# The expert stage in a hand-written instruction order, in a transformer block on one Trainium2 core

## The chip, the core and the metric

The kernel runs as one launch on one core of a Trainium2 chip. The metric is the device time of the launch in microseconds (us). Before the change three runs took 2419.74, 2420.95 and 2422.48 us; the median is 2420.95 us. Engines are named as in the profile: PE is the matrix engine (PEld its weight loads), DVE the vector engine, ACT the scalar engine, POOL the general-purpose engine, SP the engine that issues most DMAs.

## What is computed

The reference is one encoder layer on 1024 tokens of width 1024. The first part (three kinds of attention or recurrence, a merge and an output projection) isn't touched. The second part is a mixture of 16 experts, in which each expert chooses 128 tokens:

```python
def expert_choice_ffn(h, w_router, w_gate, w_up, w_down):
    affinity = jax.nn.softmax((h @ w_router).astype(jnp.float32), axis=-1)
    top_val, top_idx = lax.top_k(affinity.transpose(0, 2, 1), cap)          # cap = 128
    xe = jax.vmap(lambda hb, ib: hb[ib])(h, top_idx)
    act = jax.nn.silu(einsum(xe, w_gate)) * einsum(xe, w_up)                # 1024 -> 2048
    ye = einsum(act, w_down) * top_val[..., None]                           # 2048 -> 1024
    # scatter-add of ye to the rows top_idx; then x + that sum, and a final rms_norm
```

All tensors are float32. The three weight matrices of one expert hold 8 MB each, so the 16 experts read 384 pieces of 1 MB.

## The kernel before

**Arithmetic.** A float32 product is made of three matmuls in the type fp32r. Each operand is split into a high part (`hi`, a rounded copy, made by ACT) and a low part (`lo = raw - hi`, made by DVE), and high·high, low·high and high·low are added up in one PSUM bank (`mm3`, L220 to L223).

**Pieces.** The weights of one expert come in 24 pieces of 128 x 2048 numbers (1 MB): for each of four quarters `f` of the hidden width two pieces of the gate matrix `wg`, two of the up matrix `wu` and two of the down matrix `wd`. A piece is fetched by SP into one of 14 raw buffers (`RAWB`, `fetch`, L1068), ACT makes its high part `ewh` (L1212), DVE its low part `ewl` (L1213); there are four buffers for each (`SPLB`). A raw buffer comes free when the low part is done; a high or low buffer comes free when PE has read it for the last time. Each piece feeds 12 matmuls of 512 columns.

**A quarter.** `gate_up` (L1267) runs 24 matmuls of the gate into bank `g`; ACT puts Silu of it into `sg` (L1303); 24 matmuls of the up matrix go into bank `u`, and DVE multiplies `sg` by it (L1309). `down` (L1273) belongs to the quarter before: PE turns `sg` round in four 128 x 128 transposes (L1277), the result is split into `ah` and `al` (L217, L218), and 24 matmuls (L1285 to L1287) add to the two banks `y`. At the end of an expert DVE scales both banks into `ye` (L1291), and POOL adds it to rows of `acc` in DRAM by an indirect DMA (L1292). `load_x` (L1252) gathers the 128 tokens of the next expert by an indirect DMA (L1254), transposes them in two groups of four (L1261) and splits them into `xh`, `xl` (L1263, L1264).

**What sets the order.** The expert stage isn't under `tc.manual_schedule()`: a planner orders the instructions of each engine from the program order, its own estimates and the free buffers. The engines then run in that fixed order and wait for each other by semaphores. The planner put some matmuls of the up matrix between the transposes and the down matmuls, and mixed the two streams. Within a piece the three kinds of matmul follow each other for each `k`, so that high and low part are both in use until the piece ends.

**The end.** After the last expert's scatter the 1024 rows of `acc` are loaded in eight tiles (L1329), normed (`final_norm`, L1318: a sum of squares on ACT, a power on POOL, a scaling on DVE) and stored; the 128 rows of the last expert are gathered, completed, normed and stored again by an indirect DMA (L1331 to L1337).

Of the kernel before, what the change touches and what calls it, by code (L numbers as in the profile page):

```python
# [25 lines left out]
F32 = mybir.dt.float32  # L26
F32R = mybir.dt.float32r
# [9 lines left out]
D = 1024  # L37
# [110 lines left out]
def block_kernel(ctx: ExitStack, tc: tile.TileContext, T, out, dbg=None, upto=99):  # L148
# [73 lines left out]
        PE.matmul(out_, ll, rh, start=False, stop=False)  # L222
        PE.matmul(out_, lh, rl, start=False, stop=(k_ == K - 1))  # L223

# [510 lines left out]
    rctx.close()  # L735
    rps_ctx.close()

# [1 line left out]
    pre_ctx.close()  # L739
    pctx.close()  # L740
    yctx = ExitStack()
# [269 lines left out]
            split_to(*(v[:, k:k + WBK] for v in w), raw[:, k:k + WBK])  # L1011
        return w

# [201 lines left out]

    early = {(n, 0, f, b): piece(n, 0, f, b, G) for n, f, b in order[:SPLB]}

    def weights(n, e, f, b, **kw):
        w = early.pop((n, e, f, b), None) or piece(n, e, f, b)
        return [v.rearrange("p (a c) -> p a c", **kw) for v in w]  # L1220

    work = [affT, affw]
    for r in range(CAP // 8):
        a, b = work[r % 2], work[(r + 1) % 2]
# [19 lines left out]
    V.tensor_copy(tvT, pi[:, 0:NE])  # L1244
    mctx.close()

    # experts
    with tc.tile_pool(name="eps", bufs=1, space=PSUM, reuse_waits="tile") as ps:
        def bank(tag, bufs):
            return ps.tile([128, 512], F32, name=tag, bufs=bufs)  # L1250

        def load_x(e):  # L1252
# [3 lines left out]
            xh = ep.tile([128, KD, 128], F32R, name="xh", bufs=2)  # L1256
            xl = ep.tile([128, KD, 128], F32R, name="xl", bufs=2)
            for b in range(2):
                p = bank("tr", 2)
                for k in range(4):  # L1260
                    PE.transpose(p[:, k * 128:(k + 1) * 128], xe[:, (4 * b + k) * 128:(4 * b + k + 1) * 128], ident)  # L1261
                p4 = p.rearrange("p (k t) -> p k t", k=4)
                A.activation(xh[:, 4 * b:4 * b + 4], p4, AF.Copy)  # L1263
                V.tensor_sub(xl[:, 4 * b:4 * b + 4], p4, xh[:, 4 * b:4 * b + 4].bitcast(F32))  # L1264
            return xh, xl

        def gate_up(e, f, nm, x, p):  # L1267
            for b in range(2):
                wh, wl = weights(nm, e, f, b, a=4)
                for k in range(4):  # L1270
                    mm3(p, 4 * b + k, KD, x[0][:, 4 * b + k], x[1][:, 4 * b + k], wh[:, k], wl[:, k])

        def down(e, f, sg, py):  # L1273
            ds = [weights("wd", e, f, b, a=2) for b in range(2)]
            pt = bank("tr", 2)
            for k in range(4):
                PE.transpose(pt[:, k * 128:(k + 1) * 128], sg[:, k * 128:(k + 1) * 128], ident)  # L1277
            ah = ep.tile([128, 4, 128], F32R, name="ah", bufs=1)
            al = ep.tile([128, 4, 128], F32R, name="al", bufs=1)
            split_to(ah, al, pt.rearrange("p (k t) -> p k t", k=4))  # L1280
            for k in range(4):
                for n in range(2):
                    o = py[n]
                    rh, rl = [d[:, k % 2, n * 512:(n + 1) * 512] for d in ds[k // 2]]
                    PE.matmul(o, ah[:, k], rh, start=(f == 0 and k == 0), stop=False)  # L1285
                    PE.matmul(o, al[:, k], rh, start=False, stop=False)  # L1286
                    PE.matmul(o, ah[:, k], rl, start=False, stop=(f == 3 and k == 3))  # L1287
            if f == 3 and e + 1 < NE:
                ye = lv.tile([128, D], F32, name="ye")
                for n in range(2):  # L1290
                    V.tensor_scalar(ye[:, n * 512:(n + 1) * 512], py[n], tvT[:, e:e + 1], None, op0=OP.mult)  # L1291
                G.indirect_dma_start(out=acc[:, :], out_offset=bass.IndirectOffsetOnAxis(ap=idx[:, e:e + 1], axis=0),  # L1292
                                     in_=ye, in_offset=None, compute_op=OP.add)

        xs = load_x(0)
        pend = py = None
        for e in range(NE):
            x = xs
            for f in range(4):
                pg, pu = bank("g", 2), bank("u", 2)  # L1300
                gate_up(e, f, "wg", x, pg)
                sg = ep.tile([128, 512], F32, name="sg", bufs=2)
                A.activation(sg, pg, AF.Silu)  # L1303
                if pend:
                    down(*pend)
                if f == 0:
                    py = [bank("y", 2) for _ in range(2)]
                gate_up(e, f, "wu", x, pu)
                V.tensor_mul(sg, sg, pu)  # L1309
                if f == 1 and e + 1 < NE:  # L1310
                    xs = load_x(e + 1)
                pend = (e, f, sg, py)
        down(*pend)

        grow = lv.tile([128, D], F32, name="xe")
        A.dma_start(grow, bass.AP(tensor=T["gfin"].tensor, offset=T["gfin"].offset, ap=[[0, 128], [1, D]]))

        def final_norm(t):  # L1318
            ss = ep.tile([128, 2], F32, name="ss", bufs=4)
            A.activation(t[:, D:], t[:, 0:D], AF.Square, accum_out=ss[:, 0:1])  # L1320
            rinv_of(ss[:, 0:1], ss[:, 1:2], 1, 1.0 / D, 1e-6)
            V.scalar_tensor_tensor(t[:, D:], t[:, 0:D], ss[:, 1:2], grow, op0=OP.mult, op1=OP.mult)
            return t[:, D:]

        last = idx[:, NE - 1:NE]
        ts = []
        for i in range(8):
            ts.append(rawt())
            SP.dma_start(ts[i][:, 0:D], acc[i * 128:(i + 1) * 128, :])  # L1329
        tl = rawt()  # L1330
        G.indirect_dma_start(out=tl[:, 0:D], out_offset=None, in_=acc[:, :],  # L1331
                             in_offset=bass.IndirectOffsetOnAxis(ap=last, axis=0))
        stores = [SP.dma_start(out[0, i * 128:(i + 1) * 128, :], final_norm(ts[i])) for i in range(8)]
        for n in range(2):
            hs = slice(n * 512, (n + 1) * 512)
            V.scalar_tensor_tensor(tl[:, hs], py[n], tvT[:, NE - 1:NE], tl[:, hs], op0=OP.mult, op1=OP.add)
# [30 lines left out]
```

## Time and profile before

| | |
|---|---|
| median of three runs | 2420.95 us |
| profiled execution, first to last instruction | 2419.1 us |
| mean granted clock of PE | 0.984 |
| first gate matmul of the expert stage | 1251.44 us |
| last up matmul of the expert stage | 2394.00 us |
| read from DRAM in the whole run | 517.56 MB |

The profiled execution's own time is its span of 2419.1 us; no other time of that execution is recorded. It lies 1.85 us below the median of the runs. Rows of a timeline give start and duration in us, then engine, line, operation, output and inputs, and in brackets the idle time before it with what ended it. Starts of matmuls follow each other more closely than their durations, because matmuls are pipelined: the spacing of starts is what a matmul costs in a stream. Rows of a window give the busy time of PE, PEld, DVE, ACT and POOL, then PE's granted clock, the busy share of the 16 DMA engines and GB/s.

### The profile page before, as it was taken

The page shows a single profiled execution, that of the slowest core. Times are in us where ns is not written, and L with a number is a line of the kernel's source. Part 1 is how long each engine was busy: PE and PEld are TensorE (multiplying, and loading weights), DVE is VectorE, ACT ScalarE, POOL GpSimd, SP SyncE. Part 2 cuts the span into 40 slices and gives each one's busy share as a digit, 9 for nine tenths or more (in the row PEclk, how much of TensorE's full clock was granted, in tenths as well). Part 3 has the DMA queues.
Part 4 walks back from the last instruction along what each step waited for, and adds up shares of the span by engine and source line. Part 5 has one row for each costly group of instructions (what it writes and reads, how often), then busy time and mean ns, then how long its engine had stood idle before and what let it go on. Part 6 is the DMA issues. An engine that isn't in the chain of part 4 may idle for free.

```text
span 2419.1 us, 34315 instructions
## 1 busy us (share of the span) xinstructions
PE 2279.5 (94%) x12931; PEld 1819.1 (75%) x12931; DVE 1725.5 (71%) x2155; ACT 1334.0 (55%) x1616; POOL 592.8 (25%) x1187
## 2 busy tenths in 40 slices
PE   7999999999999989999939999999999999999997
PEld 6677788877778767778727777777777777777775
DVE  6556556655665488762378888888888888888887
ACT  6554333333343378522236776776767667767675
POOL 1000666766666243340140000000011101011001
PEclk9999999999999999999969999999999999999998
DMA  6435443444343331363769999999999999999894
GB/s 233 151 137 209 129 122 98 117 126 125 98 119 96 122 111 64 116 191 121 250 267 372 357 367 364 355 360 375 362 370 362 361 359 374 365 375 367 295 413 173
DMA packets 193910, 588.55 MB, mean 243 GB/s; under 512 B 53072, under 2 KB 97360, under 8 KB 144592
## 3 DMA queue, kind: packets, MB, share of 16 engines
q1 hardware_dynamic: 187120, 562.88, 64.0%
q0 software_dynamic: 4752, 17.30, 2.8%
q10 hardware_dynamic: 1872, 6.17, 0.7%
q8 instruction: 102, 1.67, 0.3%
q14 instruction: 64, 0.52, 0.1%
HBM read 517.56 MB, written 68.73 MB: 242 GB/s over the span
## 4 chain that ended last, share of the span: by engine, by line
PE 64%; DVE 21%; issue 5%; ACT 4%; DMA 2%; POOL 2%; SPq 0%; POOLq 0%; DVEq 0%; ACTq 0%
PE acc L695 12%; DVE ewl L1213 8%; PE u L223 5%; PE y L1286 4%; PE y L1285 4%; PE y L1287 4%; PE u L221 3%; PE u L222 3%; PE acc L221 3%; PE acc L223 3%; PE acc L222 3%; PE g L221 3%; PE g L223 3%; PE g L222 3%; ACT ewh L1212 2%
## 5 line engine op out<-in xcount | busy, mean ns | idle before, releaser
L1213 DVE TENSOR_TENSOR ewl<-raw,ewh 128x2048 fp32r<-128x2048 f32 x380 | 861.7, 2289 | 162.0 <-ACT ewh L1212 161.8
L1212 ACT ACTIVATE ewh<-raw 128x2048 fp32r<-128x2048 f32 x384 | 732.2, 1917 | 289.0 <-PE y L1286 149.4
L223 PE MATMUL u<-ewl,xh 128*128 128x512 f32 x512 | 206.3, 403 | 23.8 <-DVE ewl L1213 22.0
L1292 POOL DMA_INDIRECT acc<-ye,idx x15 | 40.0, 2666 | 768.3 <-DVE ye L1291 768.3
L695 PE MATMUL acc<-hlo,wh 128*128 128x512 f32 x560 | 225.6, 403 | 0.0
L695 PE MATMUL acc<-hhi,wh 128*128 128x512 f32 x560 | 225.1, 402 | 0.0
L695 PE MATMUL acc<-hhi,wl 128*128 128x512 f32 x560 | 225.0, 402 | 0.0
L551 POOL TENSOR_TENSOR tmul<-tinv,blk 96x60 f32<-96x60 f32 (+24 forms) x496 | 172.1, 347 | 151.8 <-DMA blk<-ldr 114.3
L221 PE MATMUL u<-ewh,xh 128*128 128x512 f32 x512 | 205.5, 401 | 0.0
L1285 PE MATMUL y<-ewh,ah 128*128 128x512 f32 x512 | 194.7, 401 | 8.6 <-ACT ah L217 8.6
L221 PE MATMUL g<-ewh,xh 128*128 128x512 f32 x512 | 201.2, 393 | 0.0
L1286 PE MATMUL y<-ewh,al 128*128 128x512 f32 x512 | 200.4, 391 | 0.8 <-DVE al L218 0.8
L1287 PE MATMUL y<-ewl,ah 128*128 128x512 f32 x512 | 199.9, 390 | 0.0
L222 PE MATMUL u<-ewh,xl 128*128 128x512 f32 x512 | 199.9, 390 | 0.0
L223 PE MATMUL g<-ewl,xh 128*128 128x512 f32 x512 | 199.9, 390 | 0.0
L222 PE MATMUL g<-ewh,xl 128*128 128x512 f32 x512 | 199.5, 390 | 0.0
L553 POOL TENSOR_TENSOR tinv<-tinv,tmul 96x60 f32<-96x60 f32 (+24 forms) x496 | 176.2, 355 | 38.9
L223 PEld LDWEIGHTS u<-ewl,xh 128*128 128x128 f32 x512 | 96.0, 188 | 67.2 <-DVE ewl L1213 49.5
L1285 PEld LDWEIGHTS y<-ewh,ah 128*128 128x128 f32 x512 | 92.4, 189 | 42.3 <-ACT ah L217 23.7
L218 DVE TENSOR_TENSOR wl<-wraw,wh 128x1024 fp32r<-128x1024 f32 (+1 forms) x60 | 76.1, 1269 | 65.1 <-ACT wh L217 65.0
L695 PEld LDWEIGHTS acc<-hlo,wh 128*128 128x128 f32 x560 | 106.2, 190 | 20.6
L695 PEld LDWEIGHTS acc<-hhi,wl 128*128 128x128 f32 x560 | 105.9, 189 | 20.2
(309 smaller groups left out, 4409.4 us busy)
## 6 DMA issues: line engine op xcount, KB each, us to landing
raw<-in_wg_dram SPq DMA_DIRECT2D x128, 1024.0 KB
raw<-in_wu_dram SPq DMA_DIRECT2D x128, 1024.0 KB
raw<-in_wd_dram SPq DMA_DIRECT2D x128, 1024.0 KB
wraw<-in_wt_dram SPq DMA_DIRECT2D x46, 512.0 KB
pt<-pz SPq DMA_DIRECT2D x16, 768.0 KB
pgt<-po SPq DMA_DIRECT2D x48, 256.0 KB
gt<-pgt SPq DMA_DIRECT2D x16, 768.0 KB
blk<-ldr SPq DMA_DIRECT2D x64, 96.0 KB
```

Source lines behind the costliest of these rows:

```text
L218: V.tensor_sub(lo, src, hi.bitcast(F32))
L221: PE.matmul(out_, lh, rh, start=(k_ == 0), stop=False)
L222: PE.matmul(out_, ll, rh, start=False, stop=False)
L223: PE.matmul(out_, lh, rl, start=False, stop=(k_ == K - 1))
L551: G.tensor_tensor(tm[:, 0:m, 0:n], tt[:, 0:m, j:j + 1].to_broadcast([4 * NB, m, n]), lt[:, j, None, j + 1:32].to_broadcast([4 * NB, m, n]) ...
L553: G.tensor_tensor(tt[:, 0:m, j + 1:32], tt[:, 0:m, j + 1:32], tm[:, 0:m, 0:n], op=OP.add)
L695: PE.matmul(p, l[:, k], r[:, k, s0:s0 + 512], start=(k == 0 and i == 0), stop=(k == KD - 1 and i == 2))
L1212: A.activation(hi, raw, AF.Copy)
L1213: eng.tensor_tensor(lo, raw, hi.bitcast(F32), op=OP.subtract)
L1285: PE.matmul(o, ah[:, k], rh, start=(f == 0 and k == 0), stop=False)
L1286: PE.matmul(o, al[:, k], rh, start=False, stop=False)
L1287: PE.matmul(o, ah[:, k], rl, start=False, stop=(f == 3 and k == 3))
```

## The change

Only the expert stage changes. It is now written out under `tc.manual_schedule()`, so each engine runs the instructions in program order. A list `seq` fixes the order of the 384 pieces: for each step `s_` (a quarter of an expert) two gate pieces, the two down pieces of the step before, two up pieces.

- **Order on PE in a step:** first gate piece; the four transposes of the `sg` of the step before; second gate piece; both down pieces of the step before; first up piece; second up piece. In the third quarter of an expert the two groups of transposes of the next expert's tokens stand ahead of the first and of the second up piece; the gather is issued in the second quarter.
- **Order within a piece:** the eight matmuls that read the high part, then the four that read the low part.
- **Splits by hand:** after the piece with number n, ACT's high part of piece n+4 is issued (`hi_of`), DVE's low part of piece n+3 (`lo_of`), and with it SP's fetch of piece n+17 (`load`).
- **Scaling:** half of `ye` is scaled by ACT, the other half by DVE.
- **End:** the eight loads of `acc` follow the last fetches. One tile is normed in the last step but one, three in the last step, four after the transposes of the last `sg`. The row of gains is fetched in the last but two.

The numbers of matmuls, transposes, splits, bytes and buffers are the same. The diff, cut to its core:

```diff
-        def gate_up(e, f, nm, x, p):
-            for b in range(2):
-                wh, wl = weights(nm, e, f, b, a=4)
-                for k in range(4):
-                    mm3(p, 4 * b + k, KD, x[0][:, 4 * b + k], x[1][:, 4 * b + k], wh[:, k], wl[:, k])
+    with tc.tile_pool(name="eps", bufs=1, space=PSUM, reuse_waits="tile") as ps, tc.manual_schedule():
+        def hi_of(n):
+            if n < len(seq) and seq[n] not in his:
+                his[seq[n]] = hi = ep.tile([128, 2048], F32R, name="ewh", bufs=SPLB)
+                A.activation(hi, raws[seq[n]], AF.Copy)
+        def lo_of(n):
+            if n < len(seq) and seq[n] not in los:
+                los[seq[n]] = lo = ep.tile([128, 2048], F32R, name="ewl", bufs=SPLB)
+                V.tensor_sub(lo, raws.pop(seq[n]), his[seq[n]].bitcast(F32))
+            load(n + RAWB)
+        def gate_up(key, p):
...
+            for k in range(4):
+                PE.matmul(p, xh[:, 4 * b + k], wh[:, k], start=(b == 0 and k == 0), stop=False)
+                PE.matmul(p, xl[:, 4 * b + k], wh[:, k], start=False, stop=False)
+            for k in range(4):
+                PE.matmul(p, xh[:, 4 * b + k], wl[:, k], start=False, stop=(b == 1 and k == 3))
+        def down(key, a, py):
...
+            for i, (l, r) in enumerate(((ah, wh), (al, wh), (ah, wl))):
+                for k in range(2):
+                    for n in range(2):
+                        PE.matmul(py[n], l[:, 2 * b + k], r[:, k, n * 512:(n + 1) * 512], ...)
+        def scaled(e, py):
+            A.activation(ye[:, 0:512], py[0], AF.Copy, scale=tvT[:, e:e + 1])
+            V.tensor_scalar(ye[:, 512:D], py[1], tvT[:, e:e + 1], None, op0=OP.mult)
...
+        for s_ in range(steps + 1):
+            if s_ < steps:
+                gate_up(seq[at], pg)
+            if s_:
+                for k in range(4):
+                    PE.transpose(pt[:, k * 128:(k + 1) * 128], sg[:, k * 128:(k + 1) * 128], ident)
+                split_to(*a, pt.rearrange("p (k t) -> p k t", k=4))
+            if s_ == steps:
+                finish(8 - len(stores))
+            if s_ < steps:
+                hi_of(at - 1 + SPLB)
+                lo_of(at - 2 + SPLB)
+                gate_up(seq[at], pg)
+                A.activation(sg, pg, AF.Silu)
+                hi_of(at - 1 + SPLB)
+                lo_of(at - 2 + SPLB)
+            if f == 1 and e + 1 < NE:
+                gather(e + 1)
+            if s_:
+                for b in range(2):
+                    down(seq[at], a, py)
+                    hi_of(at - 1 + SPLB)
+                    lo_of(at - 2 + SPLB)
+                if pf == 3 and pe + 1 < NE:
+                    scaled(pe, py)
...
+            if f == 2 and e + 1 < NE:
+                x_half(e + 1, 0)
+            if s_ < steps:
+                gate_up(seq[at], pu)
+                hi_of(at - 1 + SPLB)
+                lo_of(at - 2 + SPLB)
+                if s_ == steps - 1:
+                    finish(1)
+                if f == 2 and e + 1 < NE:
+                    x_half(e + 1, 1)
+                gate_up(seq[at], pu)
+                V.tensor_mul(sg, sg, pu)
+                hi_of(at - 1 + SPLB)
+                lo_of(at - 2 + SPLB)
```

(`at` goes up by one after each piece.)

More of the change, by code (lines that the diff above doesn't have):

```diff
@@ L1245, in block_kernel, with load, gather @@
     mctx.close()
-    with tc.tile_pool(name="eps", bufs=1, space=PSUM, reuse_waits="tile") as ps:
+    steps = NE * 4
+    seq = []
+    for s_ in range(steps + 1):
+        if s_ < steps:
+            seq += [("wg", *divmod(s_, 4), b) for b in range(2)]
+        if s_:
+            seq += [("wd", *divmod(s_ - 1, 4), b) for b in range(2)]
+        if s_ < steps:
+            seq += [("wu", *divmod(s_, 4), b) for b in range(2)]
+    raws, his, los = {}, {}, {}
+    for k_ in seq[:RAWB]:
+        if k_ in first:
+            raws[k_] = first.pop(k_)
+    for k_, (hi, lo) in early.items():
+        his[k_], los[k_] = hi, lo
+    ts = []
+    with tc.tile_pool(name="eps", bufs=1, space=PSUM, reuse_waits="tile") as ps, tc.manual_schedule():
         def bank(tag, bufs):
             return ps.tile([128, 512], F32, name=tag, bufs=bufs)
-        def load_x(e):
+        def load(n):
+            if n < len(seq):
+                if seq[n] not in raws and seq[n] not in his:
+                    raws[seq[n]] = fetch(*seq[n])
+            elif n - len(seq) < 8:
+                i = n - len(seq)
+                ts.append(rawt())
+                SP.dma_start(ts[i][:, 0:D], acc[i * 128:(i + 1) * 128, :])
+        def hi_of(n):
[7 more added lines that the diff above has]
+            load(n + RAWB)
+        def gather(e):
             xe = lv.tile([128, D], F32, name="xe")
@@ L1295, in block_kernel @@
[L1295 to L1312, printed above, removed]
@@ new lines, in down @@
+        def down(key, a, py):
+            _, e, f, b = key
+            ah, al = a
+            wh, wl = (v.pop(key).rearrange("p (a c) -> p a c", a=2) for v in (his, los))
+            for i, (l, r) in enumerate(((ah, wh), (al, wh), (ah, wl))):
+                for k in range(2):
+                    for n in range(2):
+                        PE.matmul(py[n], l[:, 2 * b + k], r[:, k, n * 512:(n + 1) * 512],
+                                  start=(f == 0 and b == 0 and i == 0 and k == 0), stop=(f == 3 and b == 1 and i == 2 and k == 1))
@@ new lines, in scaled, with gain @@
+        def scaled(e, py):
+            ye = lv.tile([128, D], F32, name="ye")
+            A.activation(ye[:, 0:512], py[0], AF.Copy, scale=tvT[:, e:e + 1])
+            V.tensor_scalar(ye[:, 512:D], py[1], tvT[:, e:e + 1], None, op0=OP.mult)
+            G.indirect_dma_start(out=acc[:, :], out_offset=bass.IndirectOffsetOnAxis(ap=idx[:, e:e + 1], axis=0),
+                                 in_=ye, in_offset=None, compute_op=OP.add)
+        def gain():
+            t = lv.tile([128, D], F32, name="xe")
+            A.dma_start(t, bass.AP(tensor=T["gfin"].tensor, offset=T["gfin"].offset, ap=[[0, 128], [1, D]]))
+            return t
@@ L1323, in final_norm @@
             return t[:, D:]
-        last = idx[:, NE - 1:NE]
[L1326 to L1333, printed above, removed]
+        stores = []
@@ new lines, in finish @@
+        def finish(n):
+            for _ in range(n):
+                i = len(stores)
+                stores.append(SP.dma_start(out[0, i * 128:(i + 1) * 128, :], final_norm(ts[i])))
+        xin = {}
+        gather(0)
+        for n in range(SPLB + RAWB):
+            load(n)
+        for b in range(2):
+            x_half(0, b)
+        last = idx[:, NE - 1:NE]
+        at = 0
+        sg = py = None
+        for s_ in range(steps + 1):
+            e, f = divmod(s_, 4)
+            pe, pf = divmod(s_ - 1, 4)
+            if s_ < steps:
+                pg = bank("g", 2)
+                gate_up(seq[at], pg)
+                at += 1
+            if s_:
+                pt = bank("tr", 2)
+                for k in range(4):
+                    PE.transpose(pt[:, k * 128:(k + 1) * 128], sg[:, k * 128:(k + 1) * 128], ident)
+                a = [ep.tile([128, 4, 128], F32R, name=n, bufs=1) for n in ("ah", "al")]
+                split_to(*a, pt.rearrange("p (k t) -> p k t", k=4))
+            if s_ == steps:
+                finish(8 - len(stores))
+            if s_ < steps:
+                hi_of(at - 1 + SPLB)
+                lo_of(at - 2 + SPLB)
+                gate_up(seq[at], pg)
+                at += 1
+                sg = ep.tile([128, 512], F32, name="sg", bufs=2)
+                A.activation(sg, pg, AF.Silu)
[3 more added lines that the diff above has]
+                gather(e + 1)
+            if s_ == steps - 3:
+                grow = gain()
+            if s_:
+                if pf == 0:
+                    py = [bank("y", 2) for _ in range(2)]
+                for b in range(2):
+                    down(seq[at], a, py)
+                    at += 1
+                    hi_of(at - 1 + SPLB)
[3 more added lines that the diff above has]
+            if s_ == steps - 1:
+                tl = rawt()
+                G.indirect_dma_start(out=tl[:, 0:D], out_offset=None, in_=acc[:, :],
+                                     in_offset=bass.IndirectOffsetOnAxis(ap=last, axis=0))
+            if s_ >= steps - 2 and s_ < steps:
+                finish(s_ - steps + 3)
+            if f == 2 and e + 1 < NE:
+                x_half(e + 1, 0)
+            if s_ < steps:
+                pu = bank("u", 2)
+                gate_up(seq[at], pu)
+                at += 1
+                hi_of(at - 1 + SPLB)
+                lo_of(at - 2 + SPLB)
+                if s_ == steps - 1:
+                    finish(1)
+                if f == 2 and e + 1 < NE:
+                    x_half(e + 1, 1)
+                gate_up(seq[at], pu)
+                at += 1
+                V.tensor_mul(sg, sg, pu)
+                hi_of(at - 1 + SPLB)
+                lo_of(at - 2 + SPLB)
```

46 lines of the change are left out of this document (11 added, 35 removed).

## The prediction

> **What bounds the kernel now.** I read the engines' shares on the page first, then windows of one expert, then the waits, then the timelines of PE, DVE and ACT.
>
> ```profile
> PE 2279.5 (94%) x12931; PEld 1819.1 (75%) x12931; DVE 1725.5 (71%) x2155; ACT 1334.0 (55%) x1616; POOL 592.8 (25%) x1187
> ```
> ```profile
> 1766.00:1838.00 72.00, 70.52 (x315) 56.03 (x314) 61.61 (x37) 50.70 (x35) 6.46 (x2) 1.00 0.96 364
> ```
>
> In the window, one expert long, PE is busy for 70.5 of 72 us at a granted clock of 1.00, DVE for 61.6, ACT for 50.7; the DMA engines are 0.96 busy at 364 GB/s. PE looks full, but a matmul that is held up counts as busy. The expert's length comes from the scatters on POOL, its share of useful work from the spacing of matmul starts.
>
> ```profile
> 1766.27 3.38 POOL L1292 DMA_INDIRECT acc<-ye,idx  x1 [49.31 <-DVE ye L1291]
> ...
> 1981.33 3.38 POOL L1292 DMA_INDIRECT acc<-ye,idx  x1 [48.43 <-DVE ye L1291]
> ```
> ```profile
> 1857.32 0.60 PE L1261 MATMUL tr<-cst,xe 128*128 128x128 f32 x4
> 1857.68 0.48 PE L221 MATMUL g<-ewh,xh 128*128 128x512 f32 x1
> ...
> 1863.26 0.60 PE L1277 MATMUL tr<-cst,sg 128*128 128x128 f32 x4
> 1863.61 0.48 PE L221 MATMUL u<-ewh,xh 128*128 128x512 f32 x1
> 1863.93 0.39 PE L222 MATMUL u<-ewh,xl 128*128 128x512 f32 x1
> 1864.59 0.73 PE L1285 MATMUL y<-ewh,ah 128*128 128x512 f32 x2 [0.28 <-ACT ah L217]
> 1865.47 0.51 PE L223 MATMUL u<-ewl,xh 128*128 128x512 f32 x1
> ...
> 1866.28 0.39 PE L1286 MATMUL y<-ewh,al 128*128 128x512 f32 x1
> ...
> 1881.02 0.60 PE L1277 MATMUL tr<-cst,sg 128*128 128x128 f32 x4
> ```
>
> Three experts take 215.06 us, 71.69 each. A quarter, transposes to transposes, takes 1881.02 - 1863.26 = 17.76 us and has 72 matmuls. From 1866.28 on nothing is held up: 65 matmuls in 14.74 us, 0.2268 each. So 72 need 16.33, and 1.43 us are lost, all between 1863.26 and 1866.28: the transposes, then two up matmuls put in while ACT splits `ah`, a wait for `ah`, and an up matmul that waits for a low part. The waits of seven experts confirm the two releasers:
>
> ```profile
> ACT ewh L1212 <- PE y L1286: 81.0, 56, 2.2
> PEld u L223 <- DVE ewl L1213: 16.9, 28, 0.9
> PEld y L1285 <- ACT ah L217: 16.7, 28, 0.7
> ```
>
> Once in each of 28 quarters PE's weight load waits for each of them, 0.6 us a time. ACT itself waits for PE to give a high buffer back, not for a transfer: the stage is paced by PE and by the order of its stream.
>
> **The change: PE's stream.** Matmuls and transposes stay as many. The price of a group of four transposes is read where nobody waits: 0.36 us from 1857.32 to 1857.68, and the 24 gate matmuls behind it take 5.58 us (to 1863.26) instead of 24 x 0.2268 = 5.44; together 0.50. I take 0.50; the lower bound is 0.36, if the stream behind doesn't slow down. The stage's ends:
>
> ```profile
> 1251.44 0.80 PE L221 MATMUL g<-ewh,xh 128*128 128x512 f32 x1
> ```
> ```profile
> 1253.28 0.40 PE L221 MATMUL g<-ewh,xh 128*128 128x512 f32 x1
> ```
> ```profile
> 2394.00 0.39 PE L223 MATMUL u<-ewl,xh 128*128 128x512 f32 x1
> 2396.84 1.12 PE L1277 MATMUL tr<-cst,sg 128*128 128x128 f32 x4 [2.45 <-DVE sg L1309]
> ```
>
> Before, the first gate matmul to the end of the last up slot took 2394.23 - 1251.44 = 1142.8 us. After, that stretch holds 48 + 63 x 72 = 4584 matmuls (1039.7 us), 63 + 30 = 93 groups of transposes (46.5) and the slow start (four matmuls in 1.84 us instead of 0.91: 0.9): 1087.1 us, if nothing waits. Saved: 55.7.
>
> **Does anything wait?** Take a quarter with 0 at the end of the last up piece: first gate piece 0 to 2.72, transposes to 3.2, second gate piece to 5.9, down pieces to 11.4, up pieces to 16.8.
>
> ```profile
> 1863.45 0.60 ACT L1303 ACTIVATE sg<-g 128x512 f32<-128x512 f32 x1 [1.03 <-PE g L223]
> 1863.95 0.59 ACT L217 ACTIVATE ah<-tr 128x512 fp32r<-128x512 f32 x1
> ```
> ```profile
> 1868.52 1.92 ACT L1212 ACTIVATE ewh<-raw 128x2048 fp32r<-128x2048 f32 x1 [2.18 <-PE y L1286]
> ```
> ```profile
> 1875.77 0.69 DVE L1309 TENSOR_TENSOR sg<-sg,u 128x512 f32<-128x512 f32 x1 [0.28 <-PE u L223]
> 1876.38 6.69 DVE L1213 TENSOR_TENSOR ewl<-raw,ewh 128x2048 fp32r<-128x2048 f32 x3
> 1882.98 0.69 DVE L218 TENSOR_TENSOR al<-tr,ah 128x512 fp32r<-128x512 f32 x1
> ```
> ```profile
> 1907.97 1.41 DVE L1291 TENSOR_SCALAR ye<-y,tvT 128x512 f32<-128x512 f32 x2
> ```
>
> - The transposes need the product. DVE starts it some 0.25 us after the last up matmul's slot and takes 0.69: done at 1.0, needed at 2.72. The first gate piece, 12 matmuls, is the cover; without it PE would idle 1.0 us here plus 0.7 for `ah`.
> - `ah`: ACT 0.7 us behind the start of the transposes (1863.26 to 1863.95), done by 4.1, `al` by 4.8; the down pieces need them at 5.9 and 6.8.
> - A high part starts when PE has read the eighth matmul of the piece four before, 0.9 us ahead of that piece's end, and lasts 1.92; it is needed three pieces (8.2 us) after that end. On ACT a quarter holds 6 x 1.92 + 2 x 0.6 = 12.7 us of 16.8.
> - On DVE three low parts in a row take 6.69 us with the next operation 6.60 after the first: 2.20 each. A quarter holds 6 x 2.20 + 2 x 0.61 = 14.4 us, 15.6 where `xl` adds two splits of 0.61, 15.1 with the half of `ye` that stays. The queue is strictly ordered: behind `al` come the low parts of the pieces that were split high just before, the last one ends at about 15.7, 1 us before the product is due. Each low part is ready 4 us or more before its first matmul. So the waits that remain on DVE and ACT are their own idle time.
> - Moving the other half of `ye` gives ACT 0.6 us in one quarter of four, which its 4 us of room hide; were ACT full, it would cost 0.6 x 15 = 9 us. Scatter and gather keep their places, POOL has nothing else, and no other queue waits behind them.
> - SP's fetch follows each low part as before; 14 buffers are 14 x 2.8 = 39 us of work ahead.
>
> **The transfers.** Per expert 72 us x 364 GB/s = 26.2 MB.
>
> ```profile
> 1766.00:1778.00 12.00, 11.55 (x55) 9.13 (x54) 12.00 (x8) 8.09 (x7) 3.38 (x1) 1.00 0.94 304
> 1778.00:1802.00 24.00, 23.58 (x107) 18.86 (x106) 18.98 (x12) 17.21 (x12) 3.08 (x1) 1.00 1.00 413
> 1802.00:1838.00 36.00, 35.38 (x157) 28.03 (x156) 30.63 (x19) 25.39 (x17) 0.00 (x0) 1.00 0.94 350
> 2298.00:2340.00 42.00, 41.38 (x184) 33.03 (x183) 34.45 (x21) 30.12 (x19) 0.34 (x1) 1.00 1.01 420
> ```
>
> With a backlog (the last row, after SP had stood still) the same fetches beside the same splits ran at 420 GB/s for 42 us. Behind the scatter the rate falls to 304 for 12 us, which loses 12 x (1 - 304/420) = 3.3 us; then they catch up at 413, then follow the buffers at 350. The transfers need 26.2 MB / 420 + 3.3 = 65.7 us an expert, PE 288 x 0.2268 + 6 x 0.50 = 68.3. PE stays last, by 2.6 us.
>
> The Trainium skill speaks against the change here: DMA: Bandwidth & Descriptors, Where 436 GB/s comes from, lets the HBM side bind a core's loads at about 358 GB/s, with 368 as a derated figure; by 368 an expert would need 71.2 us (an estimate from that page) and the change would save next to nothing. The trace disagrees: 420 GB/s. The same skill's HBM Reference, Specifications, gives about 425 for a core that streams alone, as this one does.
>
> **The end.** Before, it took 2419.1 - 2394.2 = 24.9 us from the last up slot.
>
> ```profile
> 2404.97 0.21 DVE L196 TENSOR_SCALAR rinv_t<-ss 128x1 f32<-128x1 f32 x2
> 2405.85 2.48 DVE L1322 SCALAR_TENSOR_TENSOR raw<-raw,ss,xe 128x1024 f32<-128x1024 f32 x2 [0.67 <-POOL ss L197]
> 2408.24 1.40 DVE L1336 SCALAR_TENSOR_TENSOR raw<-y,tvT,raw 128x512 f32<-128x512 f32 x2
> ```
>
> After: product done at 1.0, `ah` at 2.4, down matmuls to about 7.9, hidden by DVE, which norms the four tiles left from about 3.3: one by one, each 0.88 (its wait for POOL) + 1.20 = 2.1, to 11.6. L1336 to the end costs 2419.1 - 2408.2 = 10.9 as before: 22.5 us, 2.4 less. If the norms of the last step hold the product back, up to 1 us of it goes.
>
> **The sum** against the profiled execution: 2419.1 - 55.7 - 2.4 = 2361.0. The median lies 1.85 above the span: 2363.
>
> **The rivals.**
> 1. *The transfers set the pace* (chance 0.13). If the busy share is a true occupancy, an expert needs 0.96 x 71.69 = 68.8 us at least, and gaps that PE no longer leaves would show as ACT waiting for `raw`: up to about 70 us, 16 x 1.7 = 27 us of the gain lost, 2390. Against it: 1.00 busy at 413 and 0.94 at 350 show that the share doesn't measure bytes. In its full form, a ceiling near today's 364 GB/s, nothing is left but the end: 2418; chance 0.03, since 420 GB/s were seen. That form is the rule of the Trainium skill's DMA: Bandwidth & Descriptors told above.
> 2. *The matmul spacing is that of a short stream* (0.14).
>
> ```profile
> 1146.01 0.39 PE L222 MATMUL acc<-wo1h,raw 128*128 128x512 f32 x1
> ```
> ```profile
> 1148.34 0.39 PE L223 MATMUL acc<-wo1l,raw 128*128 128x512 f32 x1
> ```
>
> There 10 spacings take 2.33 us, 0.233, because transposes break in every 12 matmuls. If the new order (one weight read twice in a row in `down`, banks changing each time) keeps PE at 0.233, 4584 x 0.0062 = 28 us are lost: 2391. Against it: the only breaks left are 1.5 per quarter and are priced.
> 3. *The product gets stuck in DVE's queue* (slower, 0.05). The order is fixed: if low buffers come free later than I read, the low parts ahead of the product wait for the last up piece, and the first transposes wait with all of PE behind them. One low part late (product done at 3.2) costs 0.5 us a quarter, 30 us in all. Two cost 2.7, 63 x 2.7 = 170: 2533. It turns slower than before from a product at 2.72 + 0.92 = 3.6 us after the last up matmul. For it: 1 us of room. Against: each low part waits for a piece that PE ended 2.7 us or more before.
> 4. *It doesn't do what it says* (0.03): other waits of the same 0.6 us per quarter take the place of the two, and the stretch stays: 2418 to 2425.
>
> **The numbers.** Forecast 2363, chance 0.62. The range reaches from 2350 (93 groups at 0.36 instead of 0.50: 13 us less) to 2392, which takes in the partial forms of rivals 1 and 2 and leaves out rivals 3, 4 and the full form of 1. What can be told from no change is about 0.2%, 4.8 us. Faster: 0.62 + 0.13 + 0.14 = 0.89; same: rival 4 and the full rival 1, 0.06; slower: rival 3, 0.05.
>
> **What would show it.** Right: scatters 68.3 us apart; no wait of PE for `ah` or `ewl`; starts 0.227 apart through whole quarters; DVE near 0.88 busy, waiting before the product; DMA near 385 GB/s; last up matmul near 2338. Wrong: ACT waiting for `raw` from a DMA (rival 1), spacing 0.233 (rival 2), PE waiting for `sg` ahead of the transposes (rival 3).

## The result and the profile after

The changed kernel takes 2364.93 us (median of four runs, 2364.28 to 2366.48), the kernel before beside it 2420.68 us (2419.74 to 2422.48): a ratio of 0.9766, 95% interval 0.9755 to 0.9778. The profiled execution of the changed kernel took 2365.14 us, its span is 2363.3 us. The forecast was 2363 us.

First the engines' shares on the page of the changed kernel:

```profile
PE 2251.8 (95%) x12931; PEld 1825.8 (77%) x12931; DVE 1710.3 (72%) x2140; ACT 1338.9 (57%) x1631; POOL 602.7 (26%) x1187
```

The number of matmuls is the same, PE's busy time is 27.7 us less (a matmul that is held up counts as busy). Then the scatters on POOL, one per expert, the first and the last of nine:

```profile
1738.01 2.89 POOL L1324 DMA_INDIRECT acc<-ye,idx  x1 [62.30 <-DVE ye L1323]
...
2283.13 2.89 POOL L1324 DMA_INDIRECT acc<-ye,idx  x1 [62.30 <-DVE ye L1323]
```

Eight experts take 545.12 us, 68.14 each (before 71.69). The window of one expert (busy time of PE, PEld, DVE, ACT and POOL, then PE's clock, the DMA share and GB/s):

```profile
1738.00:1806.10 68.10, 68.10 (x314) 56.37 (x313) 60.25 (x36) 50.98 (x36) 5.54 (x2) 1.00 0.99 386
```

PE is busy for all of it. The longest waits from 1700 to 2200 us (total, times, longest), but for POOL's wait for `ye`, its idle time of 436.1 us between the scatters:

```profile
ACT ah L217 <- PE tr L1365: 62.4, 29, 2.2
ACT ewh L1277 <- PE u L1306: 41.5, 59, 0.8
DVE sg L1413 <- PE u L1308: 30.7, 29, 1.3
```

No line of that answer begins with PE or PEld: both waits of 28 times 0.6 us are gone, and what waits now is ACT and DVE, for PE. A quarter on PE, from transposes to transposes, and beside it DVE's product and low part:

```profile
1793.95 0.60 PE L1365 MATMUL tr<-cst,sg 128*128 128x128 f32 x4
1794.31 0.48 PE L1305 MATMUL g<-ewh,xh 128*128 128x512 f32 x1
...
1797.16 1.07 PE L1317 MATMUL y<-ewh,ah 128*128 128x512 f32 x4
...
1802.60 0.39 PE L1305 MATMUL u<-ewh,xh 128*128 128x512 f32 x1
...
1810.77 0.60 PE L1365 MATMUL tr<-cst,sg 128*128 128x128 f32 x4
```
```profile
1791.43 0.69 DVE L1413 TENSOR_TENSOR sg<-sg,u 128x512 f32<-128x512 f32 x1 [1.29 <-PE u L1308]
...
1795.22 0.69 DVE L218 TENSOR_TENSOR al<-tr,ah 128x512 fp32r<-128x512 f32 x1 [0.90 <-ACT ah L217]
```

A quarter takes 1810.77 - 1793.95 = 16.82 us (before 17.76). The 24 down matmuls take 1802.60 - 1797.16 = 5.44 us, 0.2267 each. The product starts at 1791.43, 2.5 us ahead of the transposes that read it, and DVE had been idle for 1.29 us before: the first gate piece covers it. `al` is done at 1795.91, 1.25 us ahead of the first down matmul.

The ends of the stretch, and the tail behind it:

```profile
1250.32 0.79 PE L1305 MATMUL g<-ewh,xh 128*128 128x512 f32 x1
```
```profile
2334.49 1.07 PE L1308 MATMUL u<-ewl,xh 128*128 128x512 f32 x4
2341.29 1.12 PE L1365 MATMUL tr<-cst,sg 128*128 128x128 f32 x4 [5.74 <-DVE sg L1413]
2343.15 2.08 PE L1317 MATMUL y<-ewh,ah 128*128 128x512 f32 x4 [0.74 <-ACT ah L217]
```
```profile
2336.34 2.29 DVE L1282 TENSOR_TENSOR ewl<-raw,ewh 128x2048 fp32r<-128x2048 f32 x1
2338.54 0.15 DVE L196 TENSOR_SCALAR rinv_t<-ss 128x1 f32<-128x1 f32 x1
2339.35 1.28 DVE L1336 SCALAR_TENSOR_TENSOR raw<-raw,ss,xe 128x1024 f32<-128x1024 f32 x1 [0.66 <-POOL ss L197]
2340.55 0.68 DVE L1413 TENSOR_TENSOR sg<-sg,u 128x512 f32<-128x512 f32 x1
...
2352.49 1.40 DVE L1419 SCALAR_TENSOR_TENSOR raw<-y,tvT,raw 128x512 f32<-128x512 f32 x2
```

The last up slot ends at 2334.49 + 0.91 = 2335.40. The stretch from the first gate matmul is 1085.1 us (before 1142.8, forecast 1087.1). The end behind it is 2363.3 - 2335.4 = 27.9 us (before 24.9, forecast 22.5), and here the profile shows something new: the last product, on a strictly ordered DVE queue, stands behind a low part and three norms. It starts 5.15 us behind the up slot and not 0.25, and PE idles for 5.74 us.

### The profile page after: what moved, and what is told of

Its sections match the earlier page's. It is cut to its first block, busy times and chain, and to the rows that moved or that the text cites. A ratio compares the mean times of both kernels' runs of the same rounds, so it can differ in the third digit from the quotient of the medians.

```text
span 2363.3 us, 34407 instructions
## 1 busy us (share of the span) xinstructions
PE 2251.8 (95%) x12931; PEld 1825.8 (77%) x12931; DVE 1710.3 (72%) x2140; ACT 1338.9 (57%) x1631; POOL 602.7 (26%) x1187
## 4 chain that ended last, share of the span: by engine, by line
PE 80%; DVE 11%; DMA 2%; POOL 2%; ACT 2%; issue 2%; SPq 0%; POOLq 0%; ACTq 0%; DVEq 0%
PE y L1317 14%; PE acc L695 12%; PE g L1305 5%; PE g L1306 5%; PE g L1308 5%; PE u L1305 5%; PE u L1306 5%; PE u L1308 5%; PE acc L221 3%; PE acc L222 3%; PE acc L223 3%; PE tr L1365 1%; DVE Gst L640 1%; PE av L887 1%; DVE rsl L218 1%
## 5 line engine op out<-in xcount | busy, mean ns | idle before, releaser
L1282 DVE TENSOR_TENSOR ewl<-raw,ewh 128x2048 fp32r<-128x2048 f32 x380 | 849.8, 2284 | 6.0 <-ACT ewh L1277 6.0
L1277 ACT ACTIVATE ewh<-raw 128x2048 fp32r<-128x2048 f32 x380 | 720.9, 1915 | 113.3 <-PE u L1306 84.4
L1305 PE MATMUL g<-ewh,xh 128*128 128x512 f32 x512 | 206.5, 403 | 0.0
L1317 PE MATMUL y<-ewh,ah 128*128 128x512 f32 x512 | 138.2, 392 | 0.7 <-ACT ah L217 0.7
L1317 PE MATMUL y<-ewl,ah 128*128 128x512 f32 x512 | 137.8, 391 | 0.0
L1317 PE MATMUL y<-ewh,al 128*128 128x512 f32 x512 | 137.7, 391 | 0.0
L1308 PE MATMUL g<-ewl,xh 128*128 128x512 f32 x512 | 137.4, 390 | 0.0
L1308 PE MATMUL u<-ewl,xh 128*128 128x512 f32 x512 | 137.1, 390 | 0.0
L695 PEld LDWEIGHTS acc<-hhi,wh 128*128 128x128 f32 x560 | 105.9, 189 | 20.1
L217 ACT ACTIVATE ah<-tr 128x512 fp32r<-128x512 f32 x64 | 38.3, 598 | 143.6 <-PE tr L1365 143.6
```

Source lines behind the costliest of these rows:

```text
L695: PE.matmul(p, l[:, k], r[:, k, s0:s0 + 512], start=(k == 0 and i == 0), stop=(k == KD - 1 and i == 2))
L1277: A.activation(hi, raws[seq[n]], AF.Copy)
L1282: V.tensor_sub(lo, raws.pop(seq[n]), his[seq[n]].bitcast(F32))
L1305: PE.matmul(p, xh[:, 4 * b + k], wh[:, k], start=(b == 0 and k == 0), stop=False)
L1308: PE.matmul(p, xh[:, 4 * b + k], wl[:, k], start=False, stop=(b == 1 and k == 3))
L1317: PE.matmul(py[n], l[:, 2 * b + k], r[:, k, n * 512:(n + 1) * 512], start=(f == 0 and b == 0 and i == 0 and k == 0), stop=(f == 3 and b == ...
```

## The experiments

**Theory 1:** the gain comes from the place of the transposes, since a gate piece on either side covers the product and the `ah` split. **Theory 2** (the rival): it comes from something else in the rewrite, such as the order within a piece, the splits being issued in time, or the halves of `ye`. Later runs ask what bounds the kernel next, and why the end was mis-sized.

Between these kernels the part ahead of the expert stage is the same, and yet the first gate matmul starts anywhere from 1248.19 us (x8) to 1254.69 us (x4) in their profiles. So differences of 2 us between totals are read from stretches inside the profiles.

**x1: the transposes one piece later.**

```diff
-            if s_:
+            if s_ == steps:
                 pt = bank("tr", 2)
                 for k in range(4):
                     PE.transpose(...)
...
                 gate_up(seq[at], pg)
                 at += 1
+                if s_:
+                    pt = bank("tr", 2)
+                    for k in range(4):
+                        PE.transpose(...)
+                    a = [...]
+                    split_to(...)
```

> The changed kernel with one thing undone: the four transposes of a quarter stand behind the second gate piece, right ahead of the down pieces, so no gate piece covers the split into ah. Theory 1 (the gain is the two waits that the gate pieces cover): PE stands still from the end of the transposes until ah is there, 0.7 + 0.6 - 0.36 = 0.95 us in each of 63 quarters, 60 us: about 2425 us, PE waiting for ah about 63 times. Theory 2 (the gain comes from the order within a piece and the splits issued by hand, which stay): at most 2375 us.

Measured: 2425.77 us, ratio 1.0017 (1.0007 to 1.0027), 71.93 us an expert. One wait of PE, once a quarter, from 1700 to 2200 us, and one of these places on the timeline:

```profile
PE y L1317 <- ACT ah L217: 19.2, 28, 0.7
```
```profile
1843.79 0.60 PE L1378 MATMUL tr<-cst,sg 128*128 128x128 f32 x4
1845.07 1.20 PE L1317 MATMUL y<-ewh,ah 128*128 128x512 f32 x4 [0.69 <-ACT ah L217]
```

A quarter is (71.93 - 68.14) / 4 = 0.95 us longer: from the start of the transposes to the next matmul 1.28 us go by (1843.79 to 1845.07), where it was 0.36 with a gate piece behind them. That is 0.92 of the 0.95; the view counts 0.69 of it as idle time. The whole gain is gone with the transposes moved by one piece, all the rest of the rewrite in place. Theory 2 falls as far as it says that the rest is enough.

**x2: the transposes one piece earlier.**

```diff
-            if s_ < steps:
-                pg = bank("g", 2)
-                gate_up(seq[at], pg)
-                at += 1
             if s_:
                 pt = bank("tr", 2)
...
                 split_to(...)
+            if s_ < steps:
+                pg = bank("g", 2)
+                gate_up(seq[at], pg)
+                at += 1
```

> The changed kernel with the four transposes ahead of the first gate piece: ah is covered twice over, the product of DVE by nothing. Theory 1: PE stands still from the last up matmul until the product is done, 0.25 + 0.69 = 0.95 us in each of 63 quarters, 60 us: about 2425 us, PE waiting for sg. Theory 2: at most 2375 us.

Measured: 2429.5 us, ratio 1.0032 (1.0019 to 1.0044), 72.17 us an expert, which is 1.01 us more in each quarter.

```profile
1841.67 0.66 PE L1361 MATMUL tr<-cst,sg 128*128 128x128 f32 x4 [0.78 <-DVE sg L1413]
```

Now PE waits for the product. Between x1 and x2 both sides of the slot are measured: with no piece behind the product, or none behind the transposes, about 1 us a quarter is lost, and one piece of 2.7 us on either side is enough. A shorter cover wasn't tried. The splits issued by hand and the order of the fetches are in both runs, so they can't carry the gain alone; taken alone they weren't tested.

**x3: the order within a piece as before** (low, high and low·high mixed per `k`).

```diff
                 PE.matmul(p, xl[:, 4 * b + k], wh[:, k], start=False, stop=False)
-            for k in range(4):
                 PE.matmul(p, xh[:, 4 * b + k], wl[:, k], ...)
```

(and the same in `down`)

> The changed kernel with the old order within a piece (high x high, low x high, high x low for each k; in the down pieces for each k and half). Theory 1: the high part comes free at the eleventh matmul instead of the eighth, 0.7 us later, and is needed 7 us after that: 2365 us, within 3. Theory 2 (freeing the high part early is what carries the gain): 2400 us or more, with PE waiting for ewh or ewl.

Measured: 2367.19 us, ratio 0.9774 (0.9757 to 0.979). An expert takes 68.14 us, and PE waits for nothing from 1700 to 2200 us. In the fixed order, low parts last brings nothing.

**x5: the kernel before, with low parts last in each piece and nothing else.**

```diff
                 for k in range(4):
-                    mm3(p, 4 * b + k, KD, ...)
+                    PE.matmul(p, x[0][:, 4 * b + k], wh[:, k], ...)
+                    PE.matmul(p, x[1][:, 4 * b + k], wh[:, k], ...)
+                for k in range(4):
+                    PE.matmul(p, x[0][:, 4 * b + k], wl[:, k], ...)
```

(and the same in `down`)

> The kernel before, with one part of the change alone: within each piece the matmuls that read the low part come last. The planner still orders the rest. Theory 1 (waits for ah and for a low part behind the transposes): those waits stay, 2410 to 2425 us. Theory 2 (the order within a piece carries the gain): 2385 us or less.

Measured: 2406.36 us, ratio 0.993 (0.9915 to 0.9945); faster than theory 1's 2410 to 2425, and far from theory 2. The windows of two experts show why:

```profile
1401.30:1470.23 68.93, 68.93 (x314) 55.90 (x313) 61.69 (x37) 50.94 (x35) 4.37 (x2) 1.00 0.99 382
1820.83:1892.59 71.76, 69.25 (x313) 56.47 (x312) 61.24 (x37) 49.41 (x35) 4.36 (x2) 1.00 0.97 366
```

In the early expert the planner had set eight up matmuls between the transposes and the down matmuls (1407.43 to 1409.34 us); they cover `ah`, and the expert takes 68.93 us (72.20 in the kernel before at that place). From the sixth expert on it set none there, the wait for `ah` (0.74 us in three quarters of an expert, 0.30 in the fourth) is back, and the expert takes 71.76. So low parts last does remove the low part's wait in the planner's stream, and the copy's cover decides whether that is worth anything. For that wait this part of the rewrite and the fixed order do the same job; with the second the first is idle (x3).

**x4: the changed program, but ordered by the planner.**

```diff
-    with tc.tile_pool(name="eps", ...) as ps, tc.manual_schedule():
+    with tc.tile_pool(name="eps", ...) as ps:
```

> The changed program without the manual schedule: the planner orders it. Theory 1: the time follows the number of waits that PE has left, whatever issues the splits; if the planner keeps PE's order it is 2365 within 5, if it moves transposes or down matmuls forward it loses about 1 us per quarter, up to 2425. My guess is 2400. Theory 2 (the splits by hand carry the gain): 2400 or more in either case, also where PE's order is kept.

Measured: 2395.06 us, ratio 0.9889 (0.9872 to 0.9905), 70.5 us an expert. The planner left the transposes of the quarter between the gate pieces, but moved those of the next expert's input in between the down matmuls, and PE's weight load waits for low parts again. The rows are from two quarters that follow each other:

```profile
1847.70 1.08 PE L1317 MATMUL y<-ewh,al 128*128 128x512 f32 x4
1848.62 0.60 PE L1295 MATMUL tr<-cst,xe 128*128 128x128 f32 x4
1848.99 1.19 PE L1317 MATMUL y<-ewl,ah 128*128 128x512 f32 x4
...
1865.54 1.08 PE L1317 MATMUL y<-ewh,al 128*128 128x512 f32 x4
1866.83 1.21 PE L1317 MATMUL y<-ewl,ah 128*128 128x512 f32 x4 [0.21 <-DVE ewl L1282]
1867.88 1.09 PE L1317 MATMUL y<-ewh,ah 128*128 128x512 f32 x4
```
```profile
PEld y L1317 <- DVE ewl L1282: 14.8, 29, 0.6
```

The kernel before took 2421.92 us beside this run, 26.9 more: of the 55.8 us about half come with the rewritten program alone, and the other half only when its order is kept. The waits account for nearly all of that half. From 1865.54 to 1867.88 eight matmuls take 2.34 us instead of 1.81, so 0.53 us are lost. That happens in three of the four quarters of an expert, and once an expert the low part of an up piece costs another 0.4 to 0.5 us. Together this is 2.0 to 2.1 of the 2.3 us that an expert takes longer (70.47 against 68.14).

**x6: both halves of `ye` on DVE.**

```diff
-            A.activation(ye[:, 0:512], py[0], AF.Copy, scale=tvT[:, e:e + 1])
+            V.tensor_scalar(ye[:, 0:512], py[0], tvT[:, e:e + 1], None, op0=OP.mult)
```

> The changed kernel with both halves of ye scaled on DVE again. If DVE's idle time covers it (1 us per quarter): 2365 us, within 2. If DVE has no room and passes it on to PE: 0.7 us in each of 15 experts, 2375 us.

Measured: 2367.12 us, ratio 0.9774 (0.9761 to 0.9787), 68.14 us an expert: DVE's idle time before the product hides it.

**x7: less work for PE**, to see what is next behind it.

```diff
-                PE.matmul(p, xl[:, 4 * b + k], wh[:, k], start=False, stop=False)
...
-            for i, (l, r) in enumerate(((ah, wh), (al, wh), (ah, wl))):
+            for i, (l, r) in ((0, (ah, wh)), (2, (ah, wl))):
```

> The changed kernel without the low x high matmuls of the expert stage (a third of the stage's matmuls; that part of the computation is left out). PE then needs 192 x 0.227 + 3 = 46.5 us for an expert, so that the next limit shows. If the transfers need 26.2 MB at 420 GB/s + 3.3 us: 65.7 us an expert, 2.4 less than now, 2326 us. If the busy share of the DMA engines in the changed kernel (0.99) is a true occupancy: 67.5 us, 2355 us. If DVE is next (60.4 us busy per expert): 2241 us.

Measured: 2289.4 us, ratio 0.9453 (0.9439 to 0.9467). All the totals expected were off. A window of an early expert, one of a later expert, the two pieces of 6 us that begin 2.2 us behind the start of the scatter at 1681.82, and ACT's longest waits from 1700 to 2200 us:

```profile
1378.80:1438.30 59.50, 51.66 (x216) 39.99 (x216) 59.50 (x36) 49.39 (x36) 4.78 (x2) 0.94 1.02 411
1660.00:1723.00 63.00, 52.70 (x215) 40.61 (x214) 59.35 (x36) 51.29 (x36) 4.78 (x2) 0.92 1.01 411
1684.00:1690.00 6.00, 6.00 (x22) 4.85 (x23) 6.00 (x4) 5.51 (x5) 2.60 (x2) 0.72 1.02 376
1690.00:1696.00 6.00, 6.00 (x28) 4.77 (x26) 5.26 (x3) 1.92 (x1) 0.00 (x0) 1.00 1.02 371
```
```profile
ACT ewh L1277 <- DMA raw<-in_wg_dram: 48.4, 49, 2.9
ACT ewh L1277 <- DMA raw<-in_wd_dram: 27.2, 41, 1.6
```

The run has two parts. The first five scatters (1319.37 to 1557.31) are 59.5 us apart, and DVE is busy for all of that time: it sets the pace, near the 60.4 us expected. At 411 GB/s 59.5 us bring 24.5 MB, while an expert needs 63.95 x 411 = 26.3 MB; the difference can only come from pieces fetched earlier, of which the raw buffers hold 14 MB (an estimate from these rows). Later that stock is used up: the scatters at 1617.25 and 2000.97 lie six experts apart, 63.95 us each. ACT now waits for fetches, so the transfers set the pace there, again at 411 GB/s. They are 4.2 us an expert below PE's 68.14, and DVE is 8.6 below it. Behind the scatter the rate falls to about 374 for 12 us and not to 304: the hole costs 12 x (1 - 374/420) = 1.3 us. Most of the 3.3 us that the prediction read from the kernel before was not the transfers' own limit.

**x8: no norms in the last step** (one before it, seven behind).

```diff
-            if s_ >= steps - 2 and s_ < steps:
-                finish(s_ - steps + 3)
+            if s_ == steps - 2:
+                finish(1)
...
-                if s_ == steps - 1:
-                    finish(1)
```

> The changed kernel without norms in the last step: one before it, seven behind the last product. The last product then starts 0.25 us after the last up matmul instead of 5.2. If the chain of single norms on DVE sets the end: seven of them from 3.3 us at 2.08 each, the last expert's rows at 17.9 us instead of 17.1: 2365 to 2367 us. If the late product and PE's slow down matmuls set it: 5 us less, 2360 us.

Measured: 2365.49 us, ratio 0.9766 (0.9753 to 0.9779): no change. The last up slot ends at 2331.95 + 0.91 = 2332.86.

```profile
2333.06 0.69 DVE L1411 TENSOR_TENSOR sg<-sg,u 128x512 f32<-128x512 f32 x1 [1.29 <-PE u L1308]
...
2337.06 1.28 DVE L1336 SCALAR_TENSOR_TENSOR raw<-raw,ss,xe 128x1024 f32<-128x1024 f32 x1 [0.69 <-POOL ss L197]
...
2349.39 1.28 DVE L1336 SCALAR_TENSOR_TENSOR raw<-raw,ss,xe 128x1024 f32<-128x1024 f32 x1 [0.73 <-POOL ss L197]
2350.59 1.40 DVE L1417 SCALAR_TENSOR_TENSOR raw<-y,tvT,raw 128x512 f32<-128x512 f32 x2
```

The product is prompt, 0.2 us behind the slot, the down matmuls are done at 2340.8, and still the tile of the last expert (L1417) is reached 17.7 us behind the slot, like the 17.1 in the changed kernel: seven norms stand ahead of it, one each (2349.39 - 2337.06) / 6 = 2.06 us, of which 0.7 is DVE waiting for POOL. A prompt product bought nothing, because the three norms that were moved behind it stand ahead of the last tile all the same: what DVE's queue holds ahead of that tile sets the end.

**x9: the norms overlapped.** The square and the power of tile i+1 are issued ahead of the scaling of tile i; the norm between the last up pieces goes behind the product; one is left for the time of the last tile's square.

```diff
-                stores.append(SP.dma_start(out[...], final_norm(ts[i])))
+                while len(sqs) < min(i + 2, 8):
+                    sqs.append(square(ts[len(sqs)]))
+                stores.append(SP.dma_start(out[...], scale(ts[i], sqs[i])))
```

> The changed kernel with the final norms taken apart: the square and the inverse root of tile i+1 are issued ahead of the scaling of tile i, so that VectorE no longer waits between a norm's two steps; the norm between the last two up pieces goes behind the product, and one norm is left for the time in which the square of the last expert's tile runs. Theory (the chain of single norms, 2.1 us each on VectorE, sets the end): five norms at about 1.4 us fit beside the last transposes and down matmuls, the end behind the last up slot falls from 27.9 to about 20 us, time 2356 to 2359. Rival (the stores and the last scatter, which waits for all of them, set the end): 2363 or more.

Measured: 2363.08 us, ratio 0.9757 (0.9743 to 0.9771). The end falls to 2363.9 - 2337.8 = 26.1 us, 1.8 less and not 8: the expectation failed. Two norms still stand ahead of the last low part and the product; the second of them is the first row:

```profile
2336.54 1.29 DVE L1341 SCALAR_TENSOR_TENSOR raw<-raw,ss,xe 128x1024 f32<-128x1024 f32 x1 [0.40 <-POOL ss L197]
2337.74 2.28 DVE L1282 TENSOR_TENSOR ewl<-raw,ewh 128x2048 fp32r<-128x2048 f32 x1
```
```profile
2340.68 0.66 PE L1372 MATMUL tr<-cst,sg 128*128 128x128 f32 x4 [2.69 <-DVE sg L1418]
2342.08 2.08 PE L1317 MATMUL y<-ewh,ah 128*128 128x512 f32 x4 [0.75 <-ACT ah L217]
```
```profile
2342.00:2347.00 5.00, 4.92 (x12) 3.85 (x13) 4.22 (x7) 4.18 (x9) 2.60 (x3) 0.50 0.28 108
```

PE idles for 2.69 us, and the matmuls behind it run at a granted clock of 0.50, 0.43 to 0.47 us each: the 24 take 8.4 us instead of 5.4.

**x10: the input's transposes right behind those of the quarter.**

```diff
                 split_to(...)
+            if f >= 2 and e + 1 < NE:
+                x_half(e + 1, f - 2)
```

(and the two places ahead of the up pieces removed)

> The changed kernel with each half of the next expert's input transposed right behind the four transposes of a quarter (third and fourth quarter of an expert) and not between down and up. Theory (each switch from transposes back to matmuls costs about 0.12 us beside the transposes' own time, and two groups in a row pay it once): 30 switches fewer, 3.6 us, time 2361 to 2362. Rival (the extra time goes with the number of transposes): 2365 with no change beyond 0.05%. If the copies of the input delay the copy that down waits for, PE waits for ah come back, 0.2 to 0.7 us each, 30 of them: 2370 or more.

Measured: 2364.33 us, ratio 0.9767 (0.9753 to 0.9781); by the total it can't be told from the changed kernel, by the period it can.

```profile
1736.49 2.89 POOL L1324 DMA_INDIRECT acc<-ye,idx  x1 [62.18 <-DVE ye L1323]
...
2280.65 2.89 POOL L1324 DMA_INDIRECT acc<-ye,idx  x1 [62.18 <-DVE ye L1323]
```

544.16 / 8 = 68.02 us an expert, 0.12 less: 0.06 for each of the two joined groups, half of what was expected. PE waits for nothing from 1700 to 2200 us.

**x11: both.**

> Both edits of the two kernels before: pipelined norms at the end and input transposes right behind those of the quarter. If both theories hold the gains add, since one lies in the stage and the other behind it: 2352 to 2355. If only one holds, 2357 to 2362.

Measured: 2364.3 us, ratio 0.9764 (0.975 to 0.9777): a miss. The period is 68.02 as in x10; the end is 2360.6 - 2334.8 = 25.8 us as in x9. Both gains are there, and at 2 us each they are too small for the totals.

**x12: as x11, with no norm between the first and the last product.** One norm at once behind the product, four beside the down matmuls, two behind the last tile's sum.

> The kernel with both edits, and no final norm scaled between the first one and the last product: the product follows the last up slot at once, one norm fills the time until al, four run beside the down matmuls, one beside the square of the last expert's tile, one behind its scaling. With the norms 1.3 us each, PE at full speed in the last down piece (5.4 us) and the last scatter issued at about 15.5 us behind the last up slot, the end is 21 us (27.9 in the changed kernel), and the stage is 1.8 us shorter by the input transposes: 2354 to 2359. Rival (the end is set by the stores, which only move together): the end stays at 26 us or more, 2361 to 2365.

Measured: 2361.79 us, ratio 0.9755 (0.9742 to 0.9769). Its five runs (2360.78 to 2363.97) lie below the four of the changed kernel (2364.28 to 2366.48): some 3 us less by the medians, though the intervals of the two ratios overlap, and x9 (0.9757) can't be told from it. The last up slot ends at 2335.05, the end is 25.65 us. Again 21 was expected; the chain of waits at its end:

```profile
2337.40:2342.90 5.50, 5.50 (x24) 4.42 (x24) 4.70 (x8) 4.10 (x8) 3.46 (x4) 1.00 0.61 235
```
```profile
2350.06 1.30 DVE raw L1341
...
2351.37 2.60 DMA out_dram<-raw
```

The down matmuls run at full clock now, but the last scatter, which must follow all stores, waits for the store of the last tile normed ahead of it: it is issued at 2355.08, 20.0 us behind the slot (22.3 in the changed kernel). The limits lie one behind the other: product, clock, norms, store. Taking away one uncovers the next.

## Why the prediction was right, and where it was not

**What bounds, and what goes.** Right. Both waits are gone from every quarter. Of the 1.43 us that a quarter held beyond its 72 matmuls 0.94 went with them (17.76 to 16.82 us); the 0.49 left is the price of the transposes, taken as 0.50. The waits of the weight load, 0.6 us each, add up to more than 0.94, since they lie partly beside matmuls under way: the row at 1864.59 shows 0.28 us of idle time on PE where its weight load waited for `ah`. The cover was rightly named: without the first gate piece PE was to idle 1.0 us for the product, x2 measured 0.78; without the second 0.7 us for `ah`, x1 measured 0.69.

**PE's stream.** 1087.1 forecast, 1085.1 measured. A group of transposes costs less than the 0.50 taken: an expert of 68.14 us holds 288 x 0.2268 = 65.3 us of matmuls, which leaves 2.8 for six groups, 0.47 each. That is 93 x 0.03 = 2.8 us less. The other way, the slow start took 1.7 us and not 0.9: the first six matmuls take 3.02 us (1250.32 to 1253.34) instead of 1.36. Together this gives the 2.0 us.

**Does anything wait?** Right: DVE is busy 60.25 of 68.10 us (0.885), and waits 30.7 / 29 = 1.06 us a quarter for the last up matmul, where 1 us was forecast.

**The transfers.** The order was right, the size not: the floor is 63.95 us an expert (x7, later part) and not 65.7. The step that failed is the hole behind the scatter, taken as the transfers' own (3.3 us); with a backlog it is 1.3. Rival 1 rested on the busy share as an occupancy: the share is 0.99 at 68.14 us, and yet the same bytes went through in 63.95. Its full form, the rule of the Trainium skill's DMA: Bandwidth & Descriptors, falls in this case with 411 GB/s held for an expert.

**The end.** This term was mis-sized: 22.5 forecast, 27.9 measured. The step that failed reads "`ah` at 2.4, down matmuls to about 7.9, hidden by DVE, which norms the four tiles left from about 3.3", with up to 1 us if the norms of the last step hold the product back. They held it back by 4.9 us, DVE normed from 8.8 on, and the last tile was reached at 17.1 us and not at 11.6: 5.5 us, all of the miss. The prediction priced a norm rightly (2.1 us), but counted only the four behind the transposes; three more and a low part stand in the same queue ahead of the product. x8 shows that moving them behind the product is no way out: with seven there the end is 28.5. The prediction also took the last down matmuls at full clock. Behind the stop they took 8.3 us and not 5.4, but ended 1.0 us before DVE reached the last tile (2351.46 and 2352.49), so DVE hid it.

**The sum.** Span 2363.3 against 2361.0: +5.4 at the end, -2.0 in the stretch, and -1.1 because the stage began earlier (1250.32 for 1251.44), which the change doesn't touch. The errors cancelled in part, and that is luck: 2363 lies closer to 2364.9 than its terms do to theirs.

**The rivals.** Rival 2 (spacing 0.233): the down stream runs at 0.2267. Rival 3 (the product stuck): not in the stage, where it is 1 us early, but at the end this is what happened. Rival 4: no wait of PE took the place of the two.

## What to carry to other kernels

When PE waits for a copy of what it has just made, look for one independent piece as long as the other engine's step, and put it between; one piece on the wrong side gave back the whole gain. Two edits may remove the same wait: test each alone and in the other's absence before crediting either. Price the tail by walking each strictly ordered queue from the last bulk operation on, counting everything issued ahead of the one that others wait for.

## What the runs showed of the hardware that was not expected

- **PE's granted clock can halve behind a short stop.** The window behind the 5.74 us of idle time in the changed kernel, then transposes behind shorter stops in x11 and, twice, in x7:

```profile
2343.00:2348.00 5.00, 4.85 (x11) 3.80 (x12) 3.06 (x5) 4.25 (x9) 1.10 (x2) 0.50 0.18 70
```
```profile
2337.65 1.11 PE L1372 MATMUL tr<-cst,sg 128*128 128x128 f32 x4 [2.69 <-DVE sg L1416]
```
```profile
1380.92 0.91 PE L1364 MATMUL tr<-cst,sg 128*128 128x128 f32 x4 [2.26 <-DVE sg L1412]
...
1747.41 0.66 PE L1364 MATMUL tr<-cst,sg 128*128 128x128 f32 x4 [2.25 <-DVE sg L1412]
```

  The granted clock is 0.50, a matmul costs 0.43 to 0.47 us; in x9, after 2.69 us of idle time, it is 0.50 too; in x12, after 0.78 us, it stays at 1.00. The Trainium skill's TensorE: Matmul & The Clock Gate (What's actually happening) states half clock after an idle window of about 3.4 us. The first and the last number agree; in x9 the longest idle stretch is shorter, though with the transposes and the wait behind it 4.2 us went by with little work. In x11 the transposes themselves already take 1.11 us behind 2.69 us of idle time (granted clock 0.50 from 2337.6 to 2339.0), and 1.12 in the kernel before behind 2.45. At full clock they take 0.66, as in x9 behind the same 2.69 us. In x7 the four matmuls behind the transposes take 2.06 us in the first case and 1.17 in the second, after stops of the same length. So between about 2.3 and 2.7 us the length of the stop alone doesn't decide; what else does, no run here shows.
- **Returning from transposes.** Four transposes start 0.36 us ahead of the next matmul, and the stream behind them is slower for a while; a group of four costs 0.47 us in all, and two groups in a row save 0.06 each.
- **A DMA share of 0.99 left 6% of room**: the same fetches at 68.14 us an expert and, with less work on PE, at 63.95.
